# Weight halves from a casting transfer and an accumulating transfer, in place of a load, a rounding and a subtraction

## The chip, the core and the metric

The program runs on one core of one Trainium2 chip. The time is device time in microseconds (us) of one execution; the median of three is given with the lowest and the highest. Engines are named as the profile names them: PE (TensorE, matmuls), PEld (its weight loads), DVE (VectorE), ACT (ScalarE), POOL (GpSimd), SP (the engine that only issues transfers). A name with q (SPq, POOLq) is the engine's instruction queue.

## The reference

One decoder layer on 512 tokens of 1024 features, in float32. The input is normed and multiplied by one wide matrix. Two token mixers work on slices of the product: MoBA attention (8 heads, causal over two blocks, queries and keys normed per head) and gated linear attention, GLA (4 heads, a low-rank gate of 16 columns). Their outputs pass through gated branches and an output product, then a squared-ReLU MLP of 4096 hidden features, and a gated embedding of width 256:

```python
h = rms_norm(x, norm_mix);  u = h @ w_in            # split into q, k, v, gates
y = sigmoid(gate_a) * (o_a @ w_branch_a) + sigmoid(gate_b) * (o_b @ w_branch_b)
x = x + y @ w_out
h2 = rms_norm(x, norm_mlp)
x = x + square(relu(h2 @ w_up)) @ w_down
x = x + sigmoid(rms_norm(x, norm_ple) @ w_ple_gate) * (p @ w_ple)
```

## The kernel before

**Halves.** TensorE multiplies in a format (fp32r) that carries 12 significant bits. So every operand is held as two halves, hi (the value rounded to that format) and lo (the rest, value minus hi), and a float32 product is three matmuls: hi times hi, hi times lo, lo times hi (`mm3`, lines 99 to 103). For a feature-major product the third of the three, L103, is the first that reads the weight's lo.

**Units.** Weights come from DRAM in units of 512 KB, [128 partitions, 1024 values]. There are 163: 8 for the attention values (numbered 0 to 7 here), 16 for the query and key tiles of the eight MoBA heads (8 to 23), the small low-rank unit 24, 8 for the GLA values (25 to 32), 8 for the GLA queries and keys (33 to 40), and 122 for all that follows. A unit is 24 matmuls of 128x512, in two ticks of 12. `fetch` (L141) issues a unit's load on SP into a buffer of tag raw (three of them). `convert` (L180) takes the oldest loaded unit, gives it a hi and a lo buffer (tags whi and wlo, three each), puts the generator `halves` in front of the background jobs, and fetches the next unit. `halves` makes hi on ACT (L151, a copy that rounds) and lo on DVE (L153, raw minus hi). `convert` is called after each unit's matmuls, for the unit two further on.

**Order.** The program's order is the order of issue, and every engine takes its own instructions in that order, so an instruction that waits holds all that stand behind it on its engine. The heads' work runs as generators that emit one stage per tick (`tick`, L113). In the MoBA part POOL has four kinds of instruction, all on 128x512: in `qk_norm` the lo half of the squares (L403, tile ql) and of the normed query or key (L153, tile c), in `attention` the lo half of a head's values (L92, tile v), and in the GLA part a product (L596) and a mask (L619). PE's next stage of `qk_norm` (`mean_sq`, L275 and L276) reads ql: it stands in PE's order right behind the next unit's matmuls.

**Start.** The first two units and the eight pieces of x are loaded piece by piece on SP and split as they land.

Of the kernel before, what the change touches and what calls it, by code (L numbers as in the profile page):

```python
"""Hybrid decoder layer on one NeuronCore: MoBA attention and gated linear attention in parallel,
gated branches, a squared-ReLU MLP and a gated per-layer embedding.

Activations are kept feature-major ([feature, token]), so that each projection is
out^T = W^T act^T with W as the stationary operand; only the two value projections are
token-major.  A float32 product runs as three fp32r products of exact halves: the tensor engine
carries 12 significant bits, x = hi + lo with both halves exact, and hi*hi + hi*lo + lo*hi.
The RMS factor of a token commutes with the projection that follows and is applied to its output.

The program is in the order of issue.  The projections are cut into ticks of 12 matmuls; the work  # L10
of the attention heads runs in the background as generators that emit a stage per tick, each
stage fed by stages of earlier ticks, so that the tensor engine finds its operands ready.
"""
# [14 lines left out]
P = 128  # L28
# [9 lines left out]
# columns of the packed per-feature vectors  # L38
C_MIX, C_MLP, C_PLE, C_ON, C_Q, C_K, C_B, NCOL = 0, 8, 16, 24, 32, 33, 34, 38

# feature-major tiles of w_in in the order of use: (q, k) of each MoBA head, (q, k) of each GLA
# head, then g_r, gate_a and gate_b
# [4 lines left out]
def kernel(ctx: ExitStack, tc: tile.TileContext, xT, pT, w_in, w_val, w_glr, w2, cols,  # L47
# [24 lines left out]
    BUFS = {"e": 3, "s": 1}  # L72

# [15 lines left out]
    def split(hi, lo, src, eng=None):  # L89
        """hi + lo = src, exactly."""  # L90
        A.activation(hi, src, AF.Copy)  # L91
        (eng or V).tensor_tensor(lo, src, f32(hi), ALU.subtract)  # L92

    def scaled_split(hi, lo, x, g):
        """hi + lo = x * g, g a column."""
        A.activation(hi, x, AF.Copy, scale=g)  # L96
        V.scalar_tensor_tensor(lo, x, g, f32(hi), ALU.mult, ALU.subtract)

    def mm3(ps, a, b, start=True, stop=True):
        """ps (+)= a^T b from exact halves a = (hi, lo), b = (hi, lo)."""  # L100
        PE.matmul(ps, a[0], b[0], start=start, stop=False)  # L101
        PE.matmul(ps, a[0], b[1], start=False, stop=False)  # L102
        PE.matmul(ps, a[1], b[0], start=False, stop=stop)  # L103

# [1 line left out]
    jobs = []  # L106

    def spawn(gen, wait=0):
        """gen yields the number of ticks until its next stage; 0 is later in the same tick, when
        the others' stages of the tick have been issued."""  # L110
        jobs.append([gen, wait])
# [27 lines left out]
    stream, raws, ready = [], [], []  # L139
    fetched = [0]  # L140

    def fetch():
        if fetched[0] < len(stream):
            src = stream[fetched[0]]
            raw = wp.tile(list(src.shape), F32, tag="raw", name=nm("raw"))
            nc.sync.dma_start(out=raw, in_=src)
            raws.append(raw)
            fetched[0] += 1

# [5 lines left out]
    def low_rank(g1, g2, raw):  # L155
        # The low-rank gate takes two passes: its columns come in pairs of groups of 16, the
        # first for hi*hi + hi*lo and the second for lo*hi.  Their sum is left to the product
        # with w2, where three pairs carry hi*hi, lo*hi and hi*lo in one pass.
        g1, g2 = (g.rearrange("p k (n c) -> p k n c", c=16) for g in (g1, g2))
        for i in range(0, 8, 2):  # L160
            A.activation(g1[:, :, i], raw, AF.Copy)
            A.activation(g2[:, :, i], raw, AF.Copy)
        yield 0
        for i in range(0, 8, 2):
            V.tensor_tensor(g1[:, :, i + 1], raw, f32(g1[:, :, i]), ALU.subtract)
            V.tensor_scalar(g2[:, :, i + 1], raw, 0.0, None, ALU.mult)

    def convert():
        if raws:
            raw = raws.pop(0)  # L170
            shape = list(raw.shape)
            if shape[2] == 16:
                shape[2] = P
            hi = wp.tile(shape, F32R, tag="whi", name=nm("whi"))
            lo = wp.tile(shape, F32R, tag="wlo", name=nm("wlo"))
            ready.append((hi, lo))
            jobs.insert(0, [(low_rank if raw.shape[2] == 16 else halves)(hi, lo, raw), 0])
            fetch()

    def gemm_fm(n, act, evac, nu=1):  # L180
        """n tiles of 128 output features, [128 features, 512 tokens], each over nu units of
        [128, 8 k-tiles, 128]; act(k) are the halves of the activations' k-tile."""
        for i in range(n):
            ps = bank(accp, "acc")
            for u in range(nu):
                w = ready.pop(0)
                for half in range(2):
                    for k in range(4 * half, 4 * half + 4):
                        mm3(ps, (w[0][:, k], w[1][:, k]), act(8 * u + k),
                            u == 0 and k == 0, u == nu - 1 and k == KT - 1)  # L190
                    if half:
                        convert()
                    tick()
            evac(i, ps)

    def gemm_tm(act, evac, first=None):
        """512 output features, [128 tokens, 512 features] for each of the four tiles of tokens,
        over four units of [128, 2 k-tiles, 512]."""
# [50 lines left out]
    # the tensor engine's clock rises with use: keep it busy until the first operands are in  # L249
# [6 lines left out]
    # distance of query p of a tile to key j, counted from the first key that tile 3 sees;  # L256
    # beyond any score where the key lies ahead
# [14 lines left out]
    def mean_sq(sh, sl, n):  # L272
        """Bank whose every row holds the sum over the partitions of sh + sl, over n."""
        ps = bank()
        PE.matmul(ps, ones[n], sh, start=True, stop=False)  # L275
        PE.matmul(ps, ones[n], sl, start=False, stop=True)  # L276
        return ps

    def rsqrt_m2(ps):
        """-2 (ps + eps)^-0.5, an estimate from exp and ln with one Newton step."""  # L280
# [9 lines left out]
    def norm_end(r, s):  # L290
        """r = rsqrt(mean + eps) from the sums of squares s."""
        sh, sl = tt("qh", F32R), tt("ql", F32R)
        split(sh, sl, s)
        yield 1
        ps = mean_sq(sh, sl, D)
        yield 1
        y = yield from rsqrt_m2(ps)
        V.tensor_scalar(r, y, -0.5, None, ALU.mult)
# [21 lines left out]
    for u in range(2):  # L320
        raw = wp.tile([P, 2, 512], F32, tag="raw", name=nm("raw"))
        hi = wp.tile([P, 2, 512], F32R, tag="whi", name=nm("whi"))
        lo = wp.tile([P, 2, 512], F32R, tag="wlo", name=nm("wlo"))
# [5 lines left out]
    load_x(4)  # L329
    load_x(5)  # L330
    fetch()
    load_x(6)
    load_x(7)
# [12 lines left out]
    def first(u):  # L346
        if u == 0:
            split_first(1, 0)
            split_first(1, 1)
            fetch()  # L350
            return first_w[0][1:]
        if u == 1:
            split_x(4)
            split_x(5)
            return first_w[1][1:]
# [36 lines left out]
    # ---- MoBA: two blocks of keys, of which a query sees its own causally and all of the one  # L392
    # before, so that the selection is the whole past ----
# [28 lines left out]
    def attention(hd):  # L422
# [12 lines left out]
        def lower(i, sc):  # L435
            # t = slope * distance - score: the softmax of -t
# [100 lines left out]
    def gla_gate(hd):  # L537
        """The decays of a head, [128, 4, 512]: from the middle of the chunk to the query and
        from the key to the middle, from the chunk's start to the query, from the key to its end;
        and the decay of the whole chunk."""  # L540
# [7 lines left out]
        # log_sigmoid(z) = min(z, 0) - ln(1 + exp(-|z|))  # L548
# [51 lines left out]
    def gla(hd):  # L600
# [17 lines left out]
        # keep the sources s <= c  # L618
# [212 lines left out]
    def ple_last(w):  # L831
        """The last tile, in two halves of the tokens."""
# [17 lines left out]
def _columns(w):  # L850
    """[K, N] -> [N / 128, K / 1024, 128, 8, 128]: units of 128 columns over eight k-tiles."""
# [5 lines left out]
def _rows(w):  # L857
    """[K, N] -> [N / 512, K / 256, 128, 2, 512]: units of 512 columns over two k-tiles."""
# [53 lines left out]
```

## Time and profile before

| | |
|---|---|
| median of 3 runs | 989.24 us (988.84 to 989.52) |
| the profiled execution, first to last instruction (span) | 987.9 us |
| PE busy | 971.7 us, 98% |
| DVE busy | 546.3 us, 55% |
| ACT busy | 433.1 us, 44% |
| POOL busy | 75.9 us, 8% |
| transfers | 92.83 MB, 94 GB/s over the span |

The profile is of one execution, known by its span; the median of the runs lies 1.3 us above it. A busy time is an average over stages that have different limits, so the table by stretches of time, and the waits in a stretch, say more than the totals. Matmuls overlap in the records: one of 128x512 is shown as about 390 ns long, while the next starts 0.23 us later.

### The profile page before, as it was taken

How to read it: one execution, taken by the hardware profiler on the slowest of the kernel's cores; microseconds unless marked ns; L12 is line 12 of the kernel's file. 1: busy time of each engine (PE TensorE's matmuls, PEld its weight loads, DVE VectorE, ACT ScalarE, POOL GpSimd, SP SyncE). 2: the span in 40 equal slices, each digit the busy share in tenths (PEclk: the TensorE clock that was granted, in tenths of full speed). 3: DMA queues.
4: the chain of work that ended last, by engine and by line, in shares of the span. 5: the costliest groups of instructions: out<-in, count | busy, mean ns of one | idle time of the engine just before them, and what ended most of it. 6: DMA issues, size and time to landing. Idle time of an engine off the chain costs nothing.

```text
span 987.9 us, 11295 instructions
## 1 busy us (share of the span) xinstructions
PE 971.7 (98%) x4424; PEld 806.0 (82%) x4424; DVE 546.3 (55%) x767; ACT 433.1 (44%) x657; POOL 75.9 (8%) x61
## 2 busy tenths in 40 slices
PE   9999999899999999999999999999999999999998
PEld 7888777687888888888888888888888888888886
DVE  5469999977546773333355555443233544344364
ACT  5558777757224852222223354432112434233441
POOL 0025333300222000000000000000000000000000
PEclk9999999899999999999999999999999999999999
DMA  7221111112221233234323223323323232323231
GB/s 256 86 85 64 64 57 48 60 64 86 87 81 47 65 106 104 92 103 171 107 86 106 86 86 107 107 86 107 107 86 113 99 103 90 107 86 106 86 128 43
DMA packets 26981, 92.83 MB, mean 94 GB/s; under 512 B 3120, under 2 KB 3504, under 8 KB 26672
## 3 DMA queue, kind: packets, MB, share of 16 engines
q1 hardware_dynamic: 26784, 92.09, 28.0%
q8 instruction: 35, 0.57, 0.2%
q14 instruction: 18, 0.15, 0.1%
q10 hardware_dynamic: 144, 0.02, 0.0%
HBM read 90.00 MB, written 2.10 MB: 93 GB/s over the span
## 4 chain that ended last, share of the span: by engine, by line
PE 88%; DVE 9%; issue 2%; ACT 1%; POOL 0%; DVEq 0%; POOLq 0%
PE acc L101 27%; PE acc L103 26%; PE acc L102 26%; PE aux L102 2%; PE aux L103 2%; PE aux L101 2%; DVE c L449 1%; DVE c L441 1%; DVE a L491 1%; DVE wlo L153 1%; PE aux L642 1%; DVE y L287 1%; DVE s L425 1%; DVE w L286 1%; DVE e L417 1%
## 5 line engine op out<-in xcount | busy, mean ns | idle before, releaser
L101 PE MATMUL acc<-a,whi 128*128 128x512 f32 x1088 | 425.5, 391 | 0.0
L102 PE MATMUL acc<-a,whi 128*128 128x512 f32 x1088 | 423.7, 389 | 0.0
L103 PE MATMUL acc<-a,wlo 128*128 128x512 f32 x1088 | 423.6, 389 | 0.0
L153 DVE TENSOR_TENSOR wlo<-raw,whi 128x1024 fp32r<-128x1024 f32 x160 | 205.1, 1282 | 112.3 <-ACT whi L151 110.8
L103 PEld LDWEIGHTS acc<-a,wlo 128*128 128x128 f32 x1088 | 204.2, 188 | 43.0
L101 PEld LDWEIGHTS acc<-a,whi 128*128 128x128 f32 x1088 | 204.3, 188 | 42.0
L102 PEld LDWEIGHTS acc<-a,whi 128*128 128x128 f32 x1088 | 204.3, 188 | 42.0
L151 ACT ACTIVATE whi<-raw 128x1024 fp32r<-128x1024 f32 x160 | 167.8, 1050 | 132.8 <-PE acc L102 109.1
L764 ACT ACTIVATE e<-e 128x512 f32<-128x512 f32 x32 | 20.2, 632 | 96.2 <-DVE e L756 92.9
L92 DVE TENSOR_TENSOR a<-e,a 128x512 fp32r<-128x512 f32 x40 | 27.7, 692 | 47.2 <-ACT a L91 47.2
L96 ACT ACTIVATE a<-c,col 128x512 fp32r<-128x512 f32 x16 | 11.6, 723 | 68.2 <-DVE c L770 42.3
L756 DVE SCALAR_TENSOR_TENSOR e<-acc,R 128x512 f32<-128x512 f32 x31 | 21.4, 691 | 34.6 <-PE acc L103 34.6
L770 DVE TENSOR_TENSOR c<-acc,c 128x512 f32<-128x512 f32 x16 | 11.1, 692 | 53.2 <-PE acc L103 53.2
L91 ACT ACTIVATE a<-e 128x512 fp32r<-128x512 f32 x40 | 25.3, 632 | 32.6 <-DVE e L725 31.6
L702 ACT ACTIVATE a<-a 128x512 f32<-128x512 f32 x16 | 10.1, 632 | 61.5 <-DVE a L701 61.5
L101 PE MATMUL acc<-c,whi 128*128 128x512 f32 (+1 forms) x82 | 31.8, 388 | 0.1
L102 PE MATMUL acc<-c,whi 128*128 128x512 f32 (+1 forms) x82 | 31.5, 384 | 0.0
L103 PE MATMUL acc<-c,wlo 128*128 128x512 f32 (+1 forms) x82 | 31.5, 384 | 0.0
L403 POOL TENSOR_TENSOR ql<-q,qh 128x512 fp32r<-128x512 f32 x16 | 22.6, 1415 | 110.1 <-ACT qh L401 110.1
L286 DVE SCALAR_TENSOR_TENSOR w<-aux,w 128x512 f32<-128x512 f32 x23 | 15.7, 684 | 23.3 <-ACT w L284 23.3
L101 PE MATMUL acc<-whi,a 128*128 128x512 f32 x64 | 25.9, 405 | 2.7 <-DVE e L526 2.7
L701 DVE TENSOR_TENSOR a<-acc,R 128x512 f32<-128x512 f32 x16 | 11.1, 691 | 29.0 <-PE acc L103 29.0
(177 smaller groups left out, 1030.6 us busy)
## 6 DMA issues: line engine op xcount, KB each, us to landing
raw<-in_w_in_dram SPq DMA_DIRECT2D x48, 512.0 KB, 3.3
raw<-in_w_up_dram SPq DMA_DIRECT2D x32, 512.0 KB, 3.3
raw<-in_w_down_dram SPq DMA_DIRECT2D x32, 512.0 KB, 3.3
raw<-in_w_val_dram SPq DMA_DIRECT2D x14, 512.0 KB, 3.3
raw<-in_w_a_dram SPq DMA_DIRECT2D x8, 512.0 KB, 3.3
raw<-in_w_b_dram SPq DMA_DIRECT2D x8, 512.0 KB, 3.2
raw<-in_w_out_dram SPq DMA_DIRECT2D x8, 512.0 KB, 3.3
raw<-in_w_gate_dram SPq DMA_DIRECT2D x8, 512.0 KB, 3.4
```

The lines of the kernel that those rows point to most:

```text
L91: A.activation(hi, src, AF.Copy)
L92: (eng or V).tensor_tensor(lo, src, f32(hi), ALU.subtract)
L96: A.activation(hi, x, AF.Copy, scale=g)
L101: PE.matmul(ps, a[0], b[0], start=start, stop=False)
L102: PE.matmul(ps, a[0], b[1], start=False, stop=False)
L103: PE.matmul(ps, a[1], b[0], start=False, stop=stop)
L151: A.activation(hi, src, AF.Copy)
L153: (eng or V).tensor_tensor(lo, src, f32(hi), ALU.subtract)
L286: V.scalar_tensor_tensor(w, ps, EPS, w, ALU.add, ALU.mult)
L403: G.tensor_tensor(sl, q2, f32(sh), ALU.subtract)
L756: V.scalar_tensor_tensor(e, ps, 0.0, R1, ALU.max, ALU.mult)
L764: A.activation(e, e, AF.Square)
```

## The change

Every 512 KB unit but the first two is made in three steps. A transfer issued on POOL reads the float32 weights and writes them into the hi buffer as fp32r. ACT writes minus hi into the lo buffer. A second transfer issued on POOL reads the same weights from DRAM again and adds them onto the lo buffer. The raw buffers go; there are five hi and four lo buffers. The first two units are still loaded by SP and split by ACT and DVE, out of tiles of another pool. `convert` is called once more at the start, so that it runs one unit further ahead in the program. The low-rank unit keeps its load on SP.

```diff
+    WHI, WLO = 5, 4
...
     def fetch():
         if fetched[0] < len(stream):
             src = stream[fetched[0]]
-            raw = wp.tile(list(src.shape), F32, tag="raw", name=nm("raw"))
-            nc.sync.dma_start(out=raw, in_=src)
-            raws.append(raw)
             fetched[0] += 1
+            if src.shape[2] == 16:
+                raw = wp.tile(list(src.shape), F32, tag="rawg", name=nm("rawg"), bufs=1)
+                nc.sync.dma_start(out=raw, in_=src)
+                raws.append((raw, None))
+                return
+            hi = wp.tile(list(src.shape), F32R, tag="whi", name=nm("whi"), bufs=WHI)
+            G.dma_start(out=hi, in_=src)
+            raws.append((hi, src))
...
+    def lower_half(hi, lo, src):
+        A.activation(lo, f32(hi), AF.Copy, scale=-1.0)
+        yield 0
+        G.dma_start(out=lo, in_=src, accum_op=ALU.add)
+
     def convert():
         if raws:
-            raw = raws.pop(0)
-            shape = list(raw.shape)
-            if shape[2] == 16:
-                shape[2] = P
-            hi = wp.tile(shape, F32R, tag="whi", name=nm("whi"))
-            lo = wp.tile(shape, F32R, tag="wlo", name=nm("wlo"))
+            x, src = raws.pop(0)
+            lo = wp.tile([P, KT, P] if src is None else list(src.shape), F32R, tag="wlo",
+                         name=nm("wlo"), bufs=WLO)
+            if src is None:
+                hi = wp.tile([P, KT, P], F32R, tag="whi", name=nm("whi"), bufs=WHI)
+                job = low_rank(hi, lo, x)
+            else:
+                hi = x
+                job = lower_half(hi, lo, src)
             ready.append((hi, lo))
-            jobs.insert(0, [(low_rank if raw.shape[2] == 16 else halves)(hi, lo, raw), 0])
-            fetch()
+            jobs.insert(0, [job, 0])
+            ahead[0] += 1 if src is None else 0
+            if src is None:
+                return
+            for _ in range(1 + ahead[0]):
+                fetch()
+            ahead[0] = 0
...
-    load_x(4)
-    load_x(5)
-    fetch()
-    load_x(6)
-    load_x(7)
+    for k in range(4, KT):
+        load_x(k)
+    for _ in range(3):
+        fetch()
...
         if u == 0:
             split_first(1, 0)
             split_first(1, 1)
-            fetch()
             return first_w[0][1:]
         if u == 1:
             split_x(4)
             split_x(5)
+            convert()
             return first_w[1][1:]
```

**First place: POOL in the MoBA part.** The names end in running numbers; ql is the lo half of the squares, c and v are lo halves for the heads. Before, POOL has this:

```order
L403 TENSOR_TENSOR ql_104_671<-q2_102_669,qh_103_670 128x512 [waits PE_49,Activation_49]
L92 TENSOR_TENSOR v0_109_697<-a2_12_143,v0_109_697 128x512 [waits Activation_49]
L153 TENSOR_TENSOR c1_112_711<-y_100_664,c1_112_711 128x512 [waits Activation_49]
L403 TENSOR_TENSOR ql_128_754<-q2_126_752,qh_127_753 128x512 [waits PE_49,Activation_49]
L153 TENSOR_TENSOR c1_112_711<-y_124_747,c1_112_711 128x512 [waits Activation_49]
L403 TENSOR_TENSOR ql_141_821<-q2_139_819,qh_140_820 128x512 [waits PE_49,Activation_49]
```

With the change, in the same place (L425, L93 and L161 are the former L403, L92 and L153; L155 is the casting transfer, L180 the accumulating one; whi_97 is unit 18):

```order
L155 DMA whi_97_686<-in_w_in_dram 128x1024 [waits DMASW5_49,PE_49]
L93 TENSOR_TENSOR v0_99_691<-a2_14_147,v0_99_691 128x512 [waits Activation_49]
L180 DMA wlo_96_685<-in_w_in_dram 128x1024 [waits DMASW6_49]
L161 TENSOR_TENSOR c1_102_705<-y_91_659,c1_102_705 128x512 [waits Activation_49]
L425 TENSOR_TENSOR ql_118_748<-q2_116_746,qh_117_747 128x512 [waits Activation_49,Pool_49]
L155 DMA whi_120_771<-in_w_in_dram 128x1024 [waits DMASW7_49,PE_49]
L180 DMA wlo_119_770<-in_w_in_dram 128x1024 [waits DMASW0_49,Activation_49]
L161 TENSOR_TENSOR c1_102_705<-y_114_741,c1_102_705 128x512 [waits Activation_49]
L425 TENSOR_TENSOR ql_130_814<-q2_128_812,qh_129_813 128x512 [waits Activation_49,Pool_49]
```

Two transfers stand in front of each ql. The casting one waits for PE (PE_49): its hi buffer is the one of five units before, here that of unit 13 (whi_54), and must have been read to the end.

**The same place on PE**, with the change (before, the same order under the lines L101 to L103, L275 and L276): the last matmuls of unit 13, the norm's two, the first of unit 14:

```order
L102 MATMUL acc_105_714<-a0_3_111,whi_54_459 128x512
L103 MATMUL acc_105_714<-a1_4_112,whi_54_459 128x512
L104 MATMUL acc_105_714<-a0_3_111,wlo_75_581 128x512
L298 MATMUL aux_123_784<-qh_117_747,ones128_87 128x512 [waits Activation_49]
L299 MATMUL aux_123_784<-ql_118_748,ones128_87 128x512 [waits Pool_49]
L102 MATMUL acc_125_792<-a0_3_111,whi_59_492 128x512 [waits DMASW5_49,DVE_49]
L103 MATMUL acc_125_792<-a1_4_112,whi_59_492 128x512
L104 MATMUL acc_125_792<-a0_3_111,wlo_86_634 128x512 [waits DMASW4_49]
```

L299 reads ql_118, which POOL now makes as the fifth instruction of the piece above, behind a transfer that waits for the L103 two rows ahead of L298.

**Second place: the MLP.** Before, SP has only loads there, each waiting for DVE to have read the buffer:

```order
L146 DMA raw_804_4648<-in_w_up_dram 128x1024 [waits DMAHW1_49,DVE_49]
L146 DMA raw_809_4688<-in_w_up_dram 128x1024 [waits DMAHW2_49,DVE_49]
L146 DMA raw_814_4724<-in_w_up_dram 128x1024 [waits DMAHW3_49,DVE_49]
L146 DMA raw_819_4760<-in_w_up_dram 128x1024 [waits DMAHW4_49,DVE_49]
L146 DMA raw_824_4796<-in_w_up_dram 128x1024 [waits DMAHW5_49,DVE_49]
```

With the change POOL has these pairs (whi_717 is unit 96, wlo_716 is the lo of unit 93):

```order
L155 DMA whi_710_4522<-in_w_up_dram 128x1024 [waits DMASW5_49,PE_49]
L180 DMA wlo_709_4521<-in_w_up_dram 128x1024 [waits DMASW6_49,Activation_49]
L155 DMA whi_717_4565<-in_w_up_dram 128x1024 [waits DMASW7_49,PE_49]
L180 DMA wlo_716_4564<-in_w_up_dram 128x1024 [waits DMASW0_49,Activation_49]
L155 DMA whi_721_4604<-in_w_up_dram 128x1024 [waits DMASW1_49,PE_49]
```

and PE, at the end of unit 92 and the start of unit 93 (whi_696):

```order
L103 MATMUL acc_723_4610<-a5_669_4199,whi_692_4406 128x512
L104 MATMUL acc_723_4610<-a4_668_4198,wlo_709_4521 128x512
L102 MATMUL acc_727_4645<-a4_668_4198,whi_696_4442 128x512 [waits DMASW1_49,DVE_49]
L103 MATMUL acc_727_4645<-a5_669_4199,whi_696_4442 128x512
L104 MATMUL acc_727_4645<-a4_668_4198,wlo_716_4564 128x512 [waits DMASW0_49]
```

The accumulating transfer of unit 93 stands behind the casting one of unit 96, which takes the hi buffer of unit 91 and so waits for PE to end unit 91; PE's third matmul of unit 93 waits for that accumulating transfer to land.

## Rows read from the trace of the kernel before

**Rows 1.** The page: busy time of PE; the core's span and clock
```profile
PE 971.7 (98%) x4424; PEld 806.0 (82%) x4424; DVE 546.3 (55%) x767; ACT 433.1 (44%) x657; POOL 75.9 (8%) x61
core 0: 987.9 us, clock 0.997
```

**Rows 2.** Stretches: us, busy of PE, PEld, DVE, ACT, POOL; clock; transfers
```profile
97.00:187.00 90.00, 84.04 (x419) 69.45 (x418) 87.83 (x168) 70.64 (x149) 34.60 (x26) 1.00 0.17 57
187.00:200.00 13.00, 10.26 (x35) 8.02 (x35) 12.69 (x27) 7.97 (x18) 2.38 (x2) 0.74 0.13 42
340.00:970.00 630.00, 630.00 (x2779) 521.22 (x2778) 288.77 (x333) 221.28 (x280) 0.00 (x0) 1.00 0.30 101
```

**Rows 3.** PE's waits: us in total, times, the longest
```profile
PE aux L102 <- DVE a L153: 4.1, 6, 1.3
PE acc L101 <- DVE e L526: 2.7, 1, 2.7
```

**Rows 4.** PE in order of time around 190 us: start, duration, line
```profile
187.29 0.39 PE L103 MATMUL acc<-whi,a 128*128 128x512 f32 x1
190.42 0.79 PE L101 MATMUL acc<-whi,a 128*128 128x512 f32 x1 [2.74 <-DVE e L526]
...
196.67 0.40 PE L101 MATMUL acc<-whi,a 128*128 128x512 f32 x1
```

**Rows 5.** In order of time after 420 us: two matmuls, ACT's rounding of two units
```profile
421.09 0.39 PE L102 MATMUL acc<-c,whi 128*128 128x512 f32 x1
421.32 0.39 PE L103 MATMUL acc<-c,wlo 128*128 128x512 f32 x1
...
421.52 1.06 ACT L151 ACTIVATE whi<-raw 128x1024 fp32r<-128x1024 f32 x1 [4.33 <-PE acc L102]
426.96 1.06 ACT L151 ACTIVATE whi<-raw 128x1024 fp32r<-128x1024 f32 x1 [4.38 <-PE acc L102]
```

**Rows 6.** Costliest groups of the page: the rounding and the subtraction
```profile
L153 DVE TENSOR_TENSOR wlo<-raw,whi 128x1024 fp32r<-128x1024 f32 x160 | 205.1, 1282 | 112.3 <-ACT whi L151 110.8
L151 ACT ACTIVATE whi<-raw 128x1024 fp32r<-128x1024 f32 x160 | 167.8, 1050 | 132.8 <-PE acc L102 109.1
```

**Rows 7.** Waits of SP's queue: us in total, times, the longest
```profile
SPq L146 <- DVE wlo L153: 795.8, 147, 10.3
```

**Rows 8.** POOL's groups by line: busy us, mean ns, idle before
```profile
L153 POOL TENSOR_TENSOR c<-y,c 128x512 fp32r<-128x512 f32 x16 | 23.3, 1457 | 26.2 <-ACT c L151 23.6 <-PE aux L276 2.6
L403 POOL TENSOR_TENSOR ql<-q,qh 128x512 fp32r<-128x512 f32 x16 | 22.6, 1415 | 110.1 <-ACT qh L401 110.1
L596 POOL TENSOR_TENSOR c<-c,e 128x512 f32<-128x512 f32 x8 | 14.1, 1764 | 85.7 <-ACT whi L151 53.9 <-DVE e L594 31.7
L92 POOL TENSOR_TENSOR v<-a,v 128x512 fp32r<-128x512 f32 x8 | 11.3, 1414 | 10.0 <-ACT v L91 10.0
L619 POOL TENSOR_SCALAR_AFFINE_SELECT v<-v 128x512 f32<-128x512 f32 x4 | 2.8, 704 | 9.3 <-ACT v L616 9.3
```

**Rows 9.** Transfers: the queue's bytes and share; landing times; SP's time to issue
```profile
q1 hardware_dynamic: 26784, 92.09, 28.0%
raw<-in_w_up_dram SPq DMA_DIRECT2D x32, 512.0 KB, 3.3
c<-in_xT_dram SPq DMA_DIRECT2D x2, 1024.0 KB, 6.1
L146 SPq DMA_DIRECT2D raw<-in_w_up_dram x32: 327/328/328, 556.5 to 812.7; - x32
```

**Rows 10.** PE in order of time at the end of a query unit
```profile
147.94 1.04 PE L475 MATMUL aux<-ident,c 128*128 128x128 f32 x8
...
149.05 0.39 PE L102 MATMUL aux<-c 128*128 128x512 f32 x1
```

**Rows 11.** The chain that ended last, at 281 us: start, us
```profile
281.28 0.89 PE aux L610 x8
```

**Rows 12.** DVE's line L425: duration in ns, least, median, most
```profile
L425 DVE TENSOR_SCALAR s<-dist x8: 414/1511/1520, 79.0 to 200.4; 128x512 f32<-128x512 f32 x8
```

More of the change, by code (lines that the diff above doesn't have):

```diff
@@ L140 @@
     fetched = [0]
+    ahead = [0]
     def fetch():
@@ L320 @@
     for u in range(2):
-        raw = wp.tile([P, 2, 512], F32, tag="raw", name=nm("raw"))
-        hi = wp.tile([P, 2, 512], F32R, tag="whi", name=nm("whi"))
-        lo = wp.tile([P, 2, 512], F32R, tag="wlo", name=nm("wlo"))
+        raw = slot(f"c{u}", [P, 2, 512])
+        hi = wp.tile([P, 2, 512], F32R, tag="whi", name=nm("whi"), bufs=WHI)
+        lo = wp.tile([P, 2, 512], F32R, tag="wlo", name=nm("wlo"), bufs=WLO)
         for k in range(2):
```

## The prediction

> **What bounds the kernel now.** Read the page's busy times first. PE is busy 971.7 of 987.9 us at a mean clock of 0.997 [rows 1], so all that a change off PE can win is in the other 16 us; what it can lose has no such end. The table by stretches says where the 16 us are [rows 2]. From 340 to 970 us PE is busy for the whole 630 us at full clock: in the MLP and its neighbours nothing is ever late. From 97 to 187 us, in the attention heads, DVE is busy 87.83 of 90 us and PE idles for 90 - 84.04 = 5.96 us; from 187 to 200 us it idles another 2.74 us. The waits name DVE as what ends these idle times [rows 3]. The longest, 2.74 us before 190.42 us, is followed by a stretch at a lower clock: from 187 to 200 us the mean granted clock is 0.74, and full speed is back at 196.67 us [rows 2, 4], so the 6.25 us between ran at about half speed (1.2 for 2.4 GHz) and cost 3.1 us. So DVE holds PE back by about 5.96 + 2.74 + 3.1 = 11.8 us in the heads, and nowhere else by much.
>
> One unit takes PE 5.44 us (ACT's rounding of two successive units starts at 421.52 and 426.96 us), and a matmul starts every 0.23 us [rows 5].
>
> **What the change takes away.** DVE's subtraction, 160 times 1.28 us = 205 us [rows 6]. In the heads this frees some 2.6 us of each head's two units, and at most the 11.8 us above come back. From 340 us on it is worth nothing: PE does not wait there. ACT's work stays as it is: a negation of the same shape takes the place of the rounding, 1.05 us each [rows 6], and I cost the exchange at nothing, covered by PE's 5.44 us per unit. SP's loads go, also off the path. The values differ from before only if the transfer rounds otherwise than ACT; no duration read here hangs on a value.
>
> **What it adds: a wait in POOL's queue.** An engine takes its instructions in order, and a transfer that waits for a buffer holds the queue: SP's queue stood 795.8 us in 147 such waits [rows 7], which cost nothing, because nothing but loads was queued there. Now the load waits stand on POOL, and each is for PE: five hi buffers mean that unit n + 5 can be loaded when unit n has been read to its end. Behind it POOL has the accumulating transfer of unit n + 2, and in the heads also the work that PE asks for next.
>
> Take the end of unit 13, the first place shown with the change. PE's second norm matmul needs ql, and until PE has ended the unit, POOL does none of this: issue a casting transfer, split v, issue an accumulating transfer, split c, make ql. The three splits take 1.41, 1.46 and 1.42 us [rows 8]. Call the time in which POOL issues a transfer x. PE has two matmuls (0.45 us) to go meanwhile. It stands for 2x + 4.29 - 0.45, about 2x + 3.8 us. No row shows POOL issuing a transfer. The nearest below is SP, 0.33 us for the same 512 KB [rows 9]; from above, POOL's own pass over a 128x512 tile, 1.41 us. POOL is a programmed engine, whose shortest operation of that shape takes 0.70 us [rows 8]; I take **x = 1.0**, midway between its shortest and its usual operation, and keep 0.33 and 1.41 for the range.
>
> The other unit ends of the heads, by the same order: units 9 and 10 (casting, accumulating, ql) 2x + 1.0 each; unit 11 (with a split of c) 2x + 2.4; unit 12, where eight score matmuls cover ql, 2x + 1.0; units 13, 15, 17 and 23, 2x + 3.8 each; units 14, 16 and 18, where transposes and a first matmul cover 1.11 us more [rows 10], 2x + 0.1 each; unit 24, 2x + 0.5. After units 19 to 22 nothing is held: the low-rank unit takes no turn at a casting transfer, so the transfer in front waits there for a unit already past. Sum: 24x + 21.4, with x = 1 **45.4 us** (29.3 to 55.2).
>
> In the GLA part POOL's product of 1.76 us stands behind the same pair [rows 8], four times before PE's transposes; 0.89 us of score matmuls and a last matmul cover it [rows 11], so at most 4 x (2 + 1.76 - 0.89 - 0.23) = 10.6 us; in three of the four places the previous head's products cover more. I take **5 us** (1 to 10).
>
> Idle times of 4 us and more should bring the low clock of [rows 4]. Five unit ends qualify (11, 13, 15, 17, 23): 5 x 3.1 = **15.5 us**. The 11.8 us of DVE's are credited in full.
>
> **What it adds: a late second half.** In the MLP POOL has transfers alone, so only the accumulating one can be late. It is issued when unit n has ended, and PE needs unit n + 2's lo at its third matmul: 5.44 + 0.45 = **5.89 us** later. How long does it take? A 512 KB load lands 3.3 us after its issue; the one hardware queue moved 92.09 MB in 28.0% of the 16 engines' span, 276.6 us, so 0.52 MB keep the engines 1.57 us [rows 9]. Less SP's 0.33 us, 1.4 us are latency. In POOL's order: x for the casting transfer, 1.4 of latency, 1.57 for its data, and then the accumulating data (its own issue is over by then). These are 512 KB from DRAM plus 512 KB of lo to be read and added, so between one load's 1.57 and twice that, 3.15 us; the 1024 KB loads landed after 6.1 us against 3.3 [rows 9], so bytes do count, and I take 3.15. Together 1.0 + 1.4 + 1.57 + 3.15 = 7.1 us, 1.23 too late. PE then stands in every second unit (a wait in one gives the next its slack), so 0.61 us per unit. It concerns units 2 to 7, 25 to 34 and 43 to 162, 136 in all: 136 x 0.61 = **84 us**. In the heads the unit ends above are longer and cover it.
>
> **Sum.** 987.9 + 45.4 + 5 + 15.5 - 11.8 + 84 = 1126; the median of the runs is 1.3 us above this execution's span, so **1127 us**.
>
> **A rule weighed.** One row says how DVE and POOL disturb each other: DVE's L425 takes 414 ns at best and 1511 in the median, beside POOL's splits [rows 12]. The Trainium skill (SBUF — State Buffer, section "SBUF: two separate sides") says that a POOL-issued transfer's descriptors are written by GpSimd, which is locked out while VectorE runs an operation on both ports, so that the transfer starts late. That speaks against this change. No run here shows such a transfer. If each of the twelve held unit ends lost the 1.1 us between those two times, the sum would be 13 us higher, 1140; I leave it out, since it is within x's bounds.
>
> **The rivals.** *In time* (26%): the accumulating data moves at a load's rate, 1.57 us. Then it lands after 5.5 us, before 5.89, the MLP keeps its pace, and only the heads lose: 1127 - 84 = **1043 us**. For it: transfers used 28% of the engines' time [rows 9], so nothing else is in the way. With x = 0.33, and the clock falling four times instead of five, 1043 - 16.1 - 4 - 3.1 = 1020.
>
> *Rate-bound* (14%): the engines that add move far below a load's rate. At four times a load's data time, 6.3 us, the transfer lands after 10.3 us: 2.2 us per unit, 136 x 2.2 = 299, and **1342 us**. It decides from 3.15 us of data up. Nothing in the trace speaks for or against it; no transfer there computes.
>
> *Not held* (6%): faster. If a transfer that waits lets POOL's later instructions pass, ql is as early as now, DVE's 11.8 us come back, and the second half, issued early, is in time: 989.2 - 11.8 = **977 us**. It decides at the point where ql no longer starts after the unit's end. Against it are SP's 795.8 us of waits, after each of which the next load came late as well [rows 7].
>
> **The numbers.** My forecast has 54%. Its own bounds: x = 1.41 gives 55.2 in the heads, 10 in the GLA part and a landing after 7.5 us, 0.82 per unit or 112 in all, so 1172 us. The range must hold most of *in time* and the near part of *rate-bound*: 1025 to 1250 (at 1250 the transfer's data takes 5 us). Outside are the far part of *rate-bound* (about 8%), *not held* (6%) and the cheapest part of *in time* (2%). A measurement of this kernel tells 0.2%, 2 us, from no change. All cases but *not held* are slower by far more: slower 0.94, faster 0.05, same 0.01.
>
> **What would show it.** In the changed profile PE's waits should be led by a norm matmul (L299) behind POOL's L425, a dozen times, up to 5.8 us, the long ones followed by a stretch at the low clock; POOL's L425 should start right behind two transfers. From 340 us on PE should wait about 1.2 us in every second unit, at its third matmul (L104), for the transfer of wlo. DVE's busy time should fall by 205 us to about 340. If the L104 waits are missing, *in time* is right; if they are over 3 us, *rate-bound*; if L425 runs in the middle of a unit, my central step is wrong.

## The result, and the profile after

The changed kernel takes 1264.25 us (median of four runs, 1260.13 to 1275.87) against 989.04 us before: a ratio of 1.2802, with a 95% interval of 1.2742 to 1.2861. The forecast was slower, 1127 us, with a range up to 1250: the sign and both mechanisms came true, the size did not. The loss is 275 us where 138 were forecast. One run of the experiments below, the second of e4_heads_dve, was 2.9% longer than the first at a lower clock and is left out.

The page's busy times, and the casting and accumulating transfers as queue q0:

```profile
PE 1053.5 (83%) x4424; PEld 838.8 (66%) x4424; DVE 368.1 (29%) x607; ACT 432.0 (34%) x657; POOL 298.1 (24%) x381
...
q0 software_dynamic: 46080, 167.79, 61.6%
```

The core's span and mean granted clock:

```profile
core 0: 1265.2 us, clock 0.949
```

PE's busy time is now 83% of the span, and the clock is no longer full [rows 1]. PE stands for 1265.2 - 1053.5 = 211.7 us, where it stood for 16.2 before. PE's waits say for what (us in total, times, longest); five smaller rows of L104, one for each further weight matrix, are left out:

```profile
PE acc L104 <- DMA wlo<-in_w_up_dram: 40.2, 18, 3.0
PE acc L104 <- DMA wlo<-in_w_down_dram: 39.1, 19, 3.0
PE acc L104 <- DMA wlo<-in_w_in_dram: 30.0, 14, 5.1
PE aux L299 <- POOL ql L425: 29.9, 7, 5.1
PE acc L103 <- DMA wlo<-in_w_val_dram: 13.1, 5, 3.5
PE aux L103 <- POOL c L161: 11.8, 6, 2.7
...
PE aux L636 <- POOL c L618: 3.4, 3, 2.0
```

Three of these are the forecast's terms. The lower half is late: 145.6 us at L104 in eight rows, 76 waits, and 13.1 us at L103 of the value units, whose products have the weights on the other side. POOL's queue holds PE in the heads: 29.9 us at ql and 11.8 at c. In the GLA part it is 3.4 us. DVE, which led the waits before [rows 3], ends 0.8 us of them, beside 2.2 us at the very start that both kernels have.

The first of the forecast's places, POOL at the end of unit 13 (start, duration, line; in brackets the idle time before):

```profile
123.70 0.60 POOL L155 DMA_DIRECT2D whi<-in_w_in_dram  x1 [8.39 <-PE acc L104]
124.32 1.28 POOL L93 TENSOR_TENSOR v<-a,v 128x512 fp32r<-128x512 f32 x1
125.53 0.91 POOL L180 DMA_DIRECT2D wlo<-in_w_in_dram  x1
126.15 1.58 POOL L161 TENSOR_TENSOR c<-y,c 128x512 fp32r<-128x512 f32 x1
127.38 1.57 POOL L425 TENSOR_TENSOR ql<-q,qh 128x512 fp32r<-128x512 f32 x1
...
129.00 0.79 PE L299 MATMUL aux<-ql,ones 128*128 128x512 f32 x1 [5.14 <-POOL ql L425]
```

POOL waits 8.39 us for PE to end the unit, then does five instructions in order, and only the fifth is what PE needs. PE's next matmuls, 0.79 and 0.63 us instead of 0.39, run at the low clock.

The second place, the plain stages, on POOL and on PE (PE's first row: a wait at L104):

```profile
708.18 0.55 POOL L155 DMA_DIRECT2D whi<-in_w_up_dram  x1 [5.32 <-PE acc L104]
708.71 0.91 POOL L180 DMA_DIRECT2D wlo<-in_w_out_dram  x1
715.53 0.55 POOL L155 DMA_DIRECT2D whi<-in_w_up_dram  x1 [5.91 <-PE acc L104]
...
717.00 0.50 PE L104 MATMUL acc<-a,wlo 128*128 128x512 f32 x1 [1.08 <-DMA wlo<-in_w_out_dram]
```

A unit ends at 708.16, the next one ends at 715.5, and the lower half whose transfer POOL began to issue at 708.71 lets PE go on at 717.00: 8.8 us after the unit's end, where 5.89 were there without a stand. Landing times (us from issue, median):

```profile
whi<-in_w_up_dram POOLq DMA_DIRECT2D x32, 512.0 KB, 4.0
wlo<-in_w_up_dram POOLq DMA_DIRECT2D x32, 512.0 KB, 7.9
```

### The profile page after: what moved, and what is told of

Its sections match the earlier page's. It is cut to its first block, busy times and chain, and to the rows that moved or that the text cites. A ratio compares the mean times of both kernels' runs of the same rounds, so it can differ in the third digit from the quotient of the medians.

```text
span 1265.2 us, 11353 instructions
## 1 busy us (share of the span) xinstructions
PE 1053.5 (83%) x4424; PEld 838.8 (66%) x4424; DVE 368.1 (29%) x607; ACT 432.0 (34%) x657; POOL 298.1 (24%) x381
## 3 DMA queue, kind: packets, MB, share of 16 engines
q0 software_dynamic: 46080, 167.79, 61.6%
## 4 chain that ended last, share of the span: by engine, by line
issue 65%; POOL 19%; PE 11%; DMA 3%; DVE 0%; POOLq 0%; SPq 0%; ACT 0%; DVEq 0%
POOL wlo L180 10%; POOL whi L155 6%; PE acc L104 3%; PE acc L103 3%; PE acc L102 3%; POOL c L161 1%; DMA wlo<-in_w_up_dram 1%; POOL c L618 1%; PE aux L103 1%; PE aux L104 1%; POOL ql L425 1%; DMA wlo<-in_w_a_dram 1%; DMA wlo<-in_w_gate_dram 1%; PE aux L102 1%; POOL v L93 1%
## 5 line engine op out<-in xcount | busy, mean ns | idle before, releaser
L104 PE MATMUL acc<-a,wlo 128*128 128x512 f32 x1088 | 450.8, 414 | 133.4 <-DMA wlo<-in_w_up_dram 40.2
L102 PE MATMUL acc<-a,whi 128*128 128x512 f32 x1088 | 444.4, 408 | 0.0
L103 PE MATMUL acc<-a,whi 128*128 128x512 f32 x1088 | 439.9, 404 | 0.0
L104 PEld LDWEIGHTS acc<-a,wlo 128*128 128x128 f32 x1088 | 214.5, 197 | 208.7 <-DMA wlo<-in_w_up_dram 48.4
L103 PEld LDWEIGHTS acc<-a,whi 128*128 128x128 f32 x1088 | 215.6, 198 | 47.8
L102 PEld LDWEIGHTS acc<-a,whi 128*128 128x128 f32 x1088 | 216.6, 199 | 43.3
L178 ACT ACTIVATE wlo<-whi 128x1024 fp32r<-128x1024 f32 x160 | 167.5, 1048 | 218.5 <-PE acc L104 214.1
L155 POOL DMA_DIRECT2D whi<-in_w_in_dram x48 | 27.1, 565 | 301.8 <-PE acc L104 237.8
L155 POOL DMA_DIRECT2D whi<-in_w_down_dram x32 | 17.5, 547 | 184.3 <-PE acc L104 177.0
L155 POOL DMA_DIRECT2D whi<-in_w_up_dram x32 | 17.5, 547 | 182.6 <-PE acc L104 182.6
L778 DVE SCALAR_TENSOR_TENSOR e<-acc,R 128x512 f32<-128x512 f32 x31 | 21.4, 692 | 131.4 <-PE acc L104 131.3
L180 POOL DMA_DIRECT2D wlo<-in_w_in_dram x48 | 43.8, 912 | 0.3 <-issue 0.3
L104 PE MATMUL acc<-c,wlo 128*128 128x512 f32 (+1 forms) x82 | 33.1, 404 | 12.2 <-DMA wlo<-in_w_a_dram 10.7
L305 ACT ACTIVATE y<-aux,epsc 128x512 f32<-128x512 f32 x23 | 15.9, 690 | 79.6 <-PE aux L299 79.6
L92 ACT ACTIVATE a<-e 128x512 fp32r<-128x512 f32 x40 | 25.2, 631 | 47.3 <-DVE e L747 46.3
L93 DVE TENSOR_TENSOR a<-e,a 128x512 fp32r<-128x512 f32 x40 | 27.7, 692 | 47.1 <-ACT a L92 47.1
L103 PE MATMUL acc<-wlo,a 128*128 128x512 f32 x64 | 26.9, 421 | 13.1 <-DMA wlo<-in_w_val_dram 13.1
```

What stands on the lines that cost most here:

```text
L155: G.dma_start(out=hi, in_=src)
L178: A.activation(lo, f32(hi), AF.Copy, scale=-1.0)
L180: G.dma_start(out=lo, in_=src, accum_op=ALU.add)
L305: A.activation(y, ps, AF.Ln, bias=epsc)
L778: V.scalar_tensor_tensor(e, ps, 0.0, R1, ALU.max, ALU.mult)
```

## The experiments

The theory after this reading: the loss has two parts behind one wait. POOL issues both transfers only when PE ends a unit; so (1) the accumulating one is too late, because adding makes it slow, and (2) POOL's work for the heads is held. Low clock follows from the waits. The rivals: the transfers simply fill the engines, or the deep prefetch does harm. Ratios are of medians, against the kernel before on the same chip (988.8 to 989.3 us). PE's waits of each kernel are in the form of the table above.

**One fetch fewer at the start** (e1_lead4).

```diff
-    for _ in range(3):
+    for _ in range(2):
         fetch()
```

> One fetch fewer at the start, so the casting transfer in front of POOL's queue waits for the unit before the one that PE has just ended. Theory 'issued too late' (both transfers leave POOL only when PE ends a unit; the second lands 8.8 us after that, 5.89 us are there): it now has 5.44 us more, so PE's waits at L104 fall from 145.6 us to under 15, those at L299 from 29.9 to under 5, the low-clock stretches with them, and the time is 975 to 1010 us. Rival 'the engines are full' (the two transfers of a unit take about 1.5 + 5 us of data, more than the 5.44 us of a unit): the waits at L104 stay over 100 us and the time stays over 1130 us.

Measured: **985.33 us**, ratio 0.9966 (0.9949 to 0.9983). The 275 us are gone, and the kernel is a little faster than the one before. First what is left of L104 over the whole run, then the heads, the plain stages and one cycle of a unit in them (columns as in [rows 2]):

```profile
PE acc L103 <- DMA wlo<-in_w_val_dram: 3.1, 1, 3.1
PE acc L104 <- DMA wlo<-in_w_in_dram: 1.9, 1, 1.9
```

```profile
97.00:187.00 90.00, 88.74 (x455) 74.96 (x454) 85.65 (x170) 75.76 (x159) 52.94 (x48) 1.00 0.56 120
187.00:200.00 13.00, 12.89 (x67) 10.72 (x66) 10.29 (x21) 8.17 (x18) 3.15 (x4) 1.00 0.53 109
340.00:970.00 630.00, 628.08 (x2770) 519.42 (x2769) 144.55 (x210) 214.54 (x271) 162.99 (x226) 1.00 0.92 196
601.25:606.69 5.44, 5.44 (x26) 4.51 (x25) 1.38 (x3) 2.22 (x3) 1.44 (x3) 1.00 0.98 204
```

and the landing of the accumulating transfer:

```profile
wlo<-in_w_up_dram POOLq DMA_DIRECT2D x32, 512.0 KB, 7.8
```

The same transfers, of the same bytes, in the same order on POOL, issued one unit end earlier relative to their use, cost PE next to nothing: the engines are not too slow, though they are near it (98% busy in that unit, 92% over the plain stages). The accumulating transfer still lands 7.8 us after its issue, against 7.9; it is no faster, it only starts earlier. In the heads PE now is busy 101.6 of 103 us, where it was 94.3 [rows 2].

**The second transfer without the addition** (e2_noadd).

```diff
-        G.dma_start(out=lo, in_=src, accum_op=ALU.add)
+        G.dma_start(out=lo, in_=src)
```

> The second transfer writes the weights into lo instead of adding them: the same bytes from DRAM, no reading and adding of lo (lo then holds the weights, so the product is another one). Theory 'adding is what takes': packets go at the first transfer's rate, the second lands about 5.5 us after PE's unit end, before the 5.89, so the L104 waits fall under 20 us; the waits for ql and c on POOL stay at 30 to 45 us; time 1030 to 1070 us. Rival 'two transfers' bytes and latencies are what takes': it still lands after 7 us or later, L104 waits over 80 us, time over 1140 us.

Measured: 1050.27 us, ratio 1.0615 (1.0593 to 1.0636). Its waits (the first three rows), the page's queue and the landing time:

```profile
PE aux L299 <- POOL ql L425: 27.4, 7, 4.8
PE aux L103 <- POOL c L161: 9.6, 6, 2.3
PE acc L104 <- DMA wlo<-in_w_in_dram: 3.1, 1, 3.1
```

```profile
q0 software_dynamic: 46080, 167.79, 49.2%
...
wlo<-in_w_up_dram POOLq DMA_DIRECT2D x32, 512.0 KB, 4.5
```

The lateness is gone (7.6 us in all at L104), the held queue is not. So it is the adding that is late: it lands 7.9 us after its issue, a plain transfer in its place after 4.5. The queue rows price it: 46080 packets in 49.2% of 1047.8 us on 16 engines are 179 ns each; in the changed kernel, 61.6% of 1265.2 us, the mean is 271 ns. Half of the packets add; if the others take 179 ns there too, an adding packet takes 2 x 271 - 179 = 363 ns, twice a plain one.

**No second transfer** (e3_nosecond).

```diff
-        G.dma_start(out=lo, in_=src, accum_op=ALU.add)
```

> The second transfer is left out (lo is minus hi, the product lacks the weights' lower half). Nothing is waited for at L104. What is left is POOL's queue behind the casting transfer: waits for ql and c, each about 0.9 us shorter than in the changed kernel, 20 to 40 us in all, a few low-clock stretches: 1000 to 1035 us. If the casting transfer itself were late, the waits would move to L102 (whi) and the time would be over 1060 us.

Measured: 1021.54 us, ratio 1.0324 (1.0304 to 1.0345). The line numbers are one lower here:

```profile
PE aux L298 <- POOL ql L424: 23.4, 7, 4.2
PE aux L103 <- POOL c L161: 6.4, 6, 1.8
```

Nothing waits at L104 or for whi. One waiting transfer on POOL is enough to hold the heads for 29.8 us. Without the second issue the longest wait is 0.9 us shorter, 4.2 against 5.1, which is that issue's 0.91 us.

**POOL's work of the heads on DVE** (e4_heads_dve): ql, c, v and the GLA product.

```diff
-        G.tensor_tensor(sl, q2, f32(sh), ALU.subtract)
+        V.tensor_tensor(sl, q2, f32(sh), ALU.subtract)
...
-        G.tensor_tensor(b, b, e, ALU.mult)
+        V.tensor_tensor(b, b, e, ALU.mult)
```

> POOL's four operations of the heads (ql, c, v, and the GLA product) go to DVE, the transfers stay as changed. Theory 'two separate losses': the waits for ql, c and L618, 45.1 us, go, with some 15 us of low clock, but the second transfer's lateness, 1.5 us per unit, now also shows in the 16 units of the heads, about 24 us: 1205 to 1240 us. Rival 'POOL's waits only hid the transfers' lateness': what is won at L299 comes back at L104, and the time stays within 1255 to 1275 us.

Measured: 1190.79 us (one run), 14 us below what was expected. From 97 to 300 us, in the heads and the first GLA units, all that PE still waits for, but for one wait of 0.2 us, is:

```profile
PE acc L103 <- DMA wlo<-in_w_val_dram: 4.4, 2, 2.5
PE acc L104 <- DMA wlo<-in_w_in_dram: 3.2, 3, 2.0
```

The 45 us at ql, c and L618 are gone, and the late lower halves are all still there over the whole run: 143.9 us at L104 and 13.2 at L103, against 145.6 and 13.1. So the two losses are separate. My 24 us of lateness in the heads did not come: 5.9 us show in their first units, before 97 us, and nothing from there to the GLA units, to which the 7.6 us above belong. More of the low clock came back than the 15 us expected: it is 0.974 over 1189.1 us, 31 us of full speed lost where the change lost 64.5 (0.949 over 1265.2). Part of that lies in the plain stages, where the waits stayed: from 340 to 970 us the clock is 0.98, in the change 0.96. So the low clock cannot be worked out from the sum of the waits alone.

**One fetch fewer, and four hi buffers** (e5_lead4_hi4).

```diff
-    WHI, WLO = 5, 4
+    WHI, WLO = 4, 4
...
-    for _ in range(3):
+    for _ in range(2):
```

> The kernel with one fetch fewer at the start, and four hi buffers instead of five. The casting transfer waits again for the unit that PE has just ended, as in the changed kernel, only with one buffer and one unit of prefetch fewer. Theory 'issued too late': what counts is which unit end POOL waits for, so all of the loss comes back: 1240 to 1290 us, L104 waits 120 to 170 us. Rival 'five units of prefetch were too many for the engines or for DRAM': a shorter prefetch is no worse, 980 to 1000 us.

Measured: 1286.36 us, ratio 1.3011 (1.2898 to 1.3124): everything is back. Three of the four largest of its waits:

```profile
PE acc L104 <- DMA wlo<-in_w_up_dram: 38.0, 25, 3.1
...
PE acc L104 <- DMA wlo<-in_w_in_dram: 35.7, 14, 7.1
PE aux L299 <- POOL ql L425: 34.8, 8, 5.1
```

It fetches as few units ahead as e1 does and is as slow as the change: what decides is not the depth of the prefetch but which unit's end stands in front of POOL's queue.

**Six hi buffers, three lo buffers** (e6_hi6lo3).

```diff
-    WHI, WLO = 5, 4
+    WHI, WLO = 6, 3
```

> The changed kernel with six hi buffers and three lo buffers, the fetches at the start as changed. With six, the casting transfer waits for the unit before the one just ended, so by the theory 'issued too late' the loss is gone: 978 to 995 us, L104 waits under 15 us. ACT's negation now waits for the lo of one unit ago, which leaves the accumulating transfer some 1.1 us later than with four lo buffers. By the rival of too much prefetch: 1240 us or more.

Measured: 996.01 us, ratio 1.0070 (1.0052 to 1.0088). L104 is down to 2.0 us, as the theory has it, but the time is a microsecond above the band. What came is a wait on another queue. The first row is ACT's, the second PE's:

```profile
ACT wlo L178 <- PE acc L104: 471.1, 137, 7.8
...
PE aux L299 <- DVE ql L161: 3.3, 2, 1.7
```

With three lo buffers ACT's negation stands for PE 137 times, against 15 (53.5 us) with one fetch fewer and four lo buffers. What stands behind it on ACT comes late, and twice the mean of a norm waits for a ql that DVE made after such an ACT; a third new wait, 2.4 us, is for DVE in the GLA gate (L572). That this accounts for all of the 10.7 us to e1_lead4 is argued, not shown.

**The two transfers swapped on POOL** (e9_swap).

```diff
-    def lower_half(hi, lo, src):
+    def lower_half(hi, lo, src, n):
...
         G.dma_start(out=lo, in_=src, accum_op=ALU.add)
+        for _ in range(n):
+            fetch()
...
-                job = lower_half(hi, lo, src)
+                job = lower_half(hi, lo, src, 1 + ahead[0])
...
-            for _ in range(1 + ahead[0]):
-                fetch()
             ahead[0] = 0
```

> The changed kernel with the two transfers of a pair swapped in POOL's queue: first the accumulating one, which waits only for ACT, then the casting one, which waits for PE's unit end; buffers and prefetch as changed. Theory 'two losses behind one wait': the accumulating transfer now stands behind the casting one of the turn before, so it leaves one unit end earlier and the waits at L104 fall under 15 us; but ql and c still stand behind the casting transfer, so PE's waits at L299 and at L103 for c stay, 20 to 35 us in all (one issue of 0.91 us and some splits shorter), with a few low-clock stretches: 1005 to 1040 us. Rival 'one loss': both go, 975 to 995 us. Rival 'the prefetch is what counts, not the order': L104 stays over 100 us, 1200 us or more.

Measured: 1021.18 us, ratio 1.0319 (1.0301 to 1.0336).

```profile
PE aux L299 <- POOL ql L425: 18.2, 7, 3.0
PE aux L103 <- POOL c L161: 6.3, 6, 1.7
...
PE acc L104 <- DMA wlo<-in_w_in_dram: 1.8, 1, 1.8
```

The accumulating transfer no longer stands behind the wait of its own turn, and its lateness is gone. The heads' work still stands behind it, and 24.5 us stay. One loss was taken away alone, with buffers and prefetch as in the change.

**The start as before** (e7_start), on top of e1_lead4: units 2 and 3 are loaded by SP and split by ACT and DVE.

```diff
+    first_hi = []
...
+            elif any(src is f for f in first_hi):
+                hi = src
+                job = halves(hi, lo, x)
...
-    for k in range(4, KT):
-        load_x(k)
-    for _ in range(2):
-        fetch()
+    for u in range(2, 4):
+        load_x(2 * u)
+        load_x(2 * u + 1)
+        raw = slot(f"c{u}", [P, 2, 512])
+        nc.sync.dma_start(out=raw, in_=stream[u])
+        raws.append((raw, wp.tile([P, 2, 512], F32R, tag="whi", name=nm("whi"), bufs=WHI)))
+        first_hi.append(raws[-1][1])
+    fetched[0] = 4
```

> The kernel with one fetch fewer, and its units 2 and 3 loaded by SP and split by ACT and DVE as in the kernel before. Unit 4 began 4.95 us later there than in the kernel before (32.62 against 27.67 us), because the two casting transfers and their sums compete with the first loads. If that is the start's whole loss, 4 to 5 us come back: 979 to 982 us, 0.7 to 1.1% under the kernel before. Rival: the accumulating transfers of units 4 and 5 are late in their place, and the time stays at 984 to 987 us.

Measured: **980.14 us**, ratio 0.9914 (0.9899 to 0.9929), the fastest of all. The start, in e1_lead4 and here (columns as in [rows 2]), PE busy 54.23 and 57.06 of 60 us:

```profile
0.00:60.00 60.00, 54.23 (x227) 43.33 (x228) 17.07 (x31) 30.05 (x43) 16.16 (x29) 1.00 0.90 220
```

```profile
0.00:60.00 60.00, 57.06 (x240) 46.04 (x241) 21.33 (x36) 31.29 (x45) 14.75 (x27) 1.00 0.84 213
```

So the change's idea, DVE's subtraction given to the transfers, is worth 0.9% here once no wait is put in front of POOL's queue and the start is left alone. It was hidden under a loss thirty times as large.

## Why the prediction was right and wrong

**Where PE would wait: right.** Both mechanisms were named with their places. There are 13 held waits for the twelve unit ends that were forecast, though only seven are at L299 and six at c, and L104 leads the list, not L299. POOL's five instructions at unit 13 stand as written. x, taken as 1.0, is 0.55 us for the casting and 0.91 for the accumulating transfer, 0.73 in the mean: 2x + 3.8 then gives 5.3 us, measured 5.1; 24x + 21.4 gives 38.9, measured 41.7; forecast 45.4. The GLA part was put at 5 us and has 3.4. Of DVE's 11.8 us some 10.4 came back, as e1_lead4 shows in the heads: 7.3 us of PE's standing and the 3.1 of low clock of [rows 4].

**The failed step: "together 1.0 + 1.4 + 1.57 + 3.15 = 7.1 us, 1.23 too late".** The first transfer's part was right in its sum, 3.97 forecast and 4.0 to 4.2 measured, and that by luck: its issue took 0.55 us and not 1.0, and the time without data 2.0 us and not 1.4 (4.1 less 0.55 and the 1.57 of data). The last term was not right. The second transfer lands at 0.55 + 7.7 = 8.25 us after the unit's end (7.7 is the median of all), which is 4.2 us after the first, not 3.15. The lateness is 2.4 us, twice the forecast's, and half of it falls on each unit, since a unit that waits gives the next one its slack: 136 x 1.18 = 160 us, measured 158.7, forecast 84. The way of it was right too: 76 waits at L104, all but one in the 122 plain units that read lo there, a long one in every second unit or a shorter one in each, as around 710 us.

Adding does take about twice a plain packet's time, as I assumed: 144 packets of 363 ns on 16 engines are 3.3 us. What I missed is that the data do not keep 16 engines busy from first to last. One cycle of the changed kernel, cut at 709.6, 711.2, 713 and 715 us (columns as in [rows 2]; the last two are the transfers' share and GB/s):

```profile
708.20:709.60 1.40, 0.36 (x2) 0.00 (x0) 0.64 (x1) 0.73 (x2) 1.40 (x2) 1.00 0.21 32
709.60:711.20 1.60, 1.02 (x4) 0.86 (x5) 1.35 (x2) 1.46 (x2) 0.02 (x1) 1.00 0.95 300
711.20:713.00 1.80, 1.80 (x9) 1.50 (x8) 0.00 (x0) 0.00 (x0) 0.00 (x0) 1.00 0.58 86
713.00:715.00 2.00, 2.00 (x10) 1.65 (x9) 0.00 (x0) 0.00 (x0) 0.00 (x0) 1.00 0.81 160
715.00:717.00 2.00, 0.92 (x6) 0.42 (x4) 0.71 (x2) 0.78 (x2) 1.44 (x2) 1.00 0.35 68
```

For 1.4 us hardly anything flows; then the casting transfer's data at 300 GB/s on 95% of the engines; then the accumulating one's, at 86, 160 and 68 GB/s, with the engines 58%, 81% and 35% busy. Why the engines stand idle for so much of its first and its last stretch is open. The Trainium skill (Collectives: The Full Stack, section "The bandwidth ceiling: the fold count and why AG ≠ RS ≠ AR") says of reductions between cores that an add in a transfer needs two source reads, and so has half a copy's rate; the 363 against 179 ns agree with that for a sum into SBUF.

**The second failed step: "idle times of 4 us and more should bring the low clock".** I put it at 15.5 us, in five places of the heads. The mean clock is 0.949 over 1265.2 us, which is 64.5 us of full speed, against 3.0 before (0.997 over 987.9). From 97 to 300 us it is (columns as in [rows 2]):

```profile
97.00:300.00 203.00, 165.29 (x743) 135.77 (x743) 130.88 (x272) 120.80 (x246) 75.51 (x74) 0.92 0.43 93
```

That is 0.08 of 203 us, about 16 us: the 15.5, but by luck, since there are nine stretches at the low clock and not five, four of them after waits of 1.8 to 2.7 us. The rest of the 64.5 lies outside, most of it in the plain stages, where I had put none: waits of 2 to 3 us brought it there too. PE from a wait at 907 us on:

```profile
907.34 0.80 PE L104 MATMUL acc<-a,wlo 128*128 128x512 f32 x1 [2.98 <-DMA wlo<-in_w_down_dram]
907.93 0.63 PE L102 MATMUL acc<-a,whi 128*128 128x512 f32 x1
...
913.05 0.61 PE L102 MATMUL acc<-a,whi 128*128 128x512 f32 x1
913.48 0.42 PE L103 MATMUL acc<-a,whi 128*128 128x512 f32 x1
913.74 0.39 PE L104 MATMUL acc<-a,wlo 128*128 128x512 f32 x1
```

After a wait of 2.98 us the matmuls follow each other every 0.43 us, half speed (1.2 for 2.4 GHz), until 913.5 us. I had one example in the trace before, after 2.74 us, and set the limit at 4 us although that example lay under it. Nor did each such wait bring it: from 754 to 850 us PE waited seven times, 2.1 to 2.9 us each, at a clock of 1.00. Which of them do is open. From 676 to 730 us, with waits of 1.0 to 1.6 us such as I had forecast, the clock was 1.00 as well, so part of this miss may follow from the first.

**The sum with measured terms.** 41.7 + 3.4 + 158.7 + 61.5 (low clock, more than before) - 8.8 (DVE's waits, 9.6 before and 0.8 now) = 256.5 us, of 277.3 between the two spans. Some 16 more are the 100 waits' own edges: a matmul is shown 0.39 us long though the next could start after 0.23, so each idle time is shown 0.16 us short. About 5 us are left over.

**The rivals.** *In time* supposed an addition at a load's rate; e2_noadd is that case, and took 1050 us for its 1043. *Rate-bound* gave 1342 us from four times a load's data time, 6.3 us, and was to decide from 3.15 us up. The 4.2 us lie between the two, so by that boundary the result is on its near side; but the packets take twice and not four times, and e1_lead4 shows that the engines can carry the whole load. *Not held* is refuted by POOL's timeline. My range ended where the transfer's data takes 5 us, and it let lateness and low clock vary one at a time. Together they use it up: the measured terms alone give 987.9 + 256.5 + 1.3 = 1246 us, and the waits' edges, which no term of mine had, carry the time past 1250. (The upper case of my own forecast adds up to 1170 us, not 1172.)

**The rule weighed.** The Trainium skill (SBUF — State Buffer, section "SBUF: two separate sides") says that DVE can keep POOL from writing a transfer's descriptors. In the changed kernel's heads, where DVE is 64% busy, a casting issue takes 593 ns in the median, and 547 from 400 us on; the transfer lands after 3.9 us there and 4.1 from 400 us on. No run here shows the 1.1 us a time that I priced it at.

## What to carry to other kernels

A transfer that waits for a buffer holds everything behind it on the engine that issues it, so it belongs on a queue without other work, or must wait for something that is already over: here one fetch fewer at the start, with the same buffers, turned 28% slower into a little faster. When a transfer is both late and beside an engine under the clock's control, price the two together: 2 to 3 us that PE stood could cost it half speed for 2 to 6 us more, though not each time. And price an accumulating transfer by its landing, not its bytes: 512 KB landed after 7.7 us, where a plain one took 4.6.

## What the runs showed of the hardware

A run of POOL's splits can hold a DVE operation to its end. In the changed kernel's heads, at unit 13, DVE's scaling of a 128x256 tile began while POOL made v:

```profile
124.46 4.64 DVE L471 TENSOR_SCALAR c<-c,sm 128x256 f32<-128x256 f32 x1
```

It is shown 4.64 us long, to 129.10 us, when POOL's last split had ended; the eight of this form took 353 ns each before and 2631 now. In e4_heads_dve, where POOL has the transfers but no splits in the heads, they take 360 ns, so it is the splits that hold it and not the transfers. This form adds 18.2 us to DVE's busy time, which fell by 178 us and not by 205. PE did not wait for it. The forecast had a row of this direction [rows 12], but weighed only the other, DVE holding POOL.

Issuing an accumulating transfer keeps POOL 0.91 us; the same one without the addition took 0.54 us in e2_noadd.
